# Memory loaded already transposed, its normalisation moved behind the key and value projections, in a one-layer hybrid decoder kernel

## The chip, the core and the metric

The kernel runs on one core of a Trainium2 chip. The metric is the device time of one execution in microseconds (us). The core has five engines with instruction queues of their own: TensorE (PE, the matrix products; its weight loads are shown as PEld), VectorE (DVE), ScalarE (ACT), GpSimd (POOL) and SyncE (SP, which here only issues DMA transfers). Each works through its queue strictly in order and waits on semaphores for the others. Matrix products accumulate in PSUM banks; everything else lives in the on-chip SBUF.

## The reference

One decoder layer over 1024 tokens of width 1024: a mixer (pooling and gated linear attention), a cross-attention over 256 memory tokens, a convolutional feed-forward part, each on an RMS-normalised input. The part that the change touches is the memory side of the cross-attention:

```python
def rms_norm(x, w):
    y = x32 * lax.rsqrt(jnp.mean(x32 * x32, axis=-1, keepdims=True) + EPS)
    return (y * w.astype(jnp.float32)).astype(x.dtype)

def memory_cross_attention(h, mem_n, wq, wkv, wo):      # mem_n = rms_norm(mem, norm_mem_w)
    q = (h @ wq).reshape(b, s, XATTN_HEADS, XATTN_HEAD_DIM)
    kv = mem_n @ wkv
    k = kv[..., :D_MODEL]; v = kv[..., D_MODEL:]
    ...
```

The inverse root mean square of a memory token is one factor for a whole row of `mem_n`. It can therefore be applied before the product with `wkv` or after it.

## The kernel before

Float32 products are made of three passes: every operand is split into a high part (a copy in the type fp32r) and a low part (the rest), and `mm3` (L89 to L92) issues high x high, high x low and low x high. `split` (L94) makes the two parts: ACT writes the high one (L96, or L99 where a row factor is given as scale), DVE the low one (L97, or L100). `wunit` (L114) does the same for half a weight chunk: ACT at L122, DVE at L123. So every K chunk needs two ACT and two DVE instructions of 128x512 before TensorE can use it.

**The head of the program.** The keys K and values V of the memory come first, because their input is small: `mem` is 256 x 1024. The two row tiles of `mem` are loaded; ACT squares and sums each row (L297, `inv_rms`), POOL adds EPS and takes the power -0.5 (L298, L299), DVE multiplies by the row factor and the gain `norm_mem_w` (L514; the gain was spread over the partitions by two products with a row of ones, L507); TensorE turns the result round in 128x128 blocks against an identity (`put_T`, L307, transposes at L312), and `split` writes it into `att["m"]`, the operand that all key and value products share.

Then `J["km"]` makes K feature block by feature block: eight blocks f0 to f7, each of 24 matmuls of 128x256 into one PSUM bank of the pool `psA` (5 banks), each with a 512 KB chunk of `wkv`. `kmem_evac` (L446) splits the bank into `att["K"]`. `J["vm"]` makes V: two halves of 48 matmuls of 128x512, from eight more chunks of 512 KB. K is not read before the cross-attention, far later.

Between these products stands other work for which the mixer waits: four token tiles of `x` (x0 to x3) are normalised by `normed` (ACT L297, POOL L298 and L299, DVE L304), transposed on TensorE (two groups of four transposes for a tile, L312, into the 3 banks of the pool `psB`) and split into `hmix[0]` (L96, L97). The order on each engine is fixed when the program is built: a scheduler places the instructions, and `pin` holds some of them in the order in which they are written. All loads of the head go through the DMA queue of SP in the order written. After V comes `J["vg", 0]`, the first product of the mixer, and from there on the program is a long stream of products.

Names in the rows: `pa` a bank of psA, `pb` of psB, `w` a split weight half, `r` a split operand, `f` a large SBUF tile, `t` a small one, `s` a column of row factors.

Of the kernel before, what the change touches and what calls it, by code (L numbers as in the profile page):

```python
# [8 lines left out]
F32 = mybir.dt.float32  # L9
F32R = mybir.dt.float32r  # L10
AF = mybir.ActivationFunctionType
ALU = mybir.AluOpType
# [3 lines left out]
P = 128  # L16
T = 1024
D = 1024
KT = D // P
TB = 512  # L20
NB = T // TB
M = 256
DFF = 2816
NF = DFF // P
EPS = 1e-6
WINDOWS = (2, 4, 8, 16)
HALO = 16
HK = KT // 2
# [13 lines left out]
@with_exitstack  # L42
def hybrid_layer(ctx: ExitStack, tc: tile.TileContext, x, mem, norm_mix_w, w_in, pool_w, pool_scale,
                 gk_w2, gk_b, gla_norm_w, w_out, norm_xattn_w, norm_mem_w, wq, wkv, wo,
                 norm_ffn_w, w_up, conv_w, conv_b, w_down, norm_final_w, out):
    nc = tc.nc

    const = ctx.enter_context(tc.tile_pool(name="const", bufs=1))
# [9 lines left out]
    pin = tc.keep_in_program_order  # L58
# [3 lines left out]
    def nm(s):  # L62
        uid[0] += 1
        return f"{s}{uid[0]}"

    def f4(*shape):
        return big.tile([P, *shape], F32, tag="big", name=nm("f"))

    def r4(*shape):
        return big.tile([P, *shape], F32R, tag="big", name=nm("r"))  # L70
# [4 lines left out]
    def sc(n):  # L75
        return small.tile([P, n], F32, tag="small", name=nm("s"))

    def bankA():
        return psA.tile([P, 512], F32, tag="psA", name=nm("pa"))

    def bankB():
        return psB.tile([P, 512], F32, tag="psB", name=nm("pb"))
# [11 lines left out]
    def split(dst, src, scale=None):  # L94
        if scale is None:
            nc.scalar.activation(dst.hi, src, AF.Copy)  # L96
            nc.vector.tensor_tensor(dst.lo, src, dst.hi.bitcast(F32), ALU.subtract)  # L97
        else:
            nc.scalar.activation(dst.hi, src, AF.Copy, scale=scale)  # L99
            nc.vector.scalar_tensor_tensor(dst.lo, src, scale, dst.hi.bitcast(F32), ALU.mult, ALU.subtract)  # L100
# [46 lines left out]
    early, issues = [False], []  # L147
# [19 lines left out]
    ws = Stream()  # L167
# [57 lines left out]
    def proj_tok(banks, feat, nk, step_k, n):  # L225
        for kc in range(0, nk, step_k // 2):
            w = ws.take()
            for i, ps in enumerate(banks):
                for kk in range(step_k // 2):
                    a = feat.k(kc + kk)  # L230
                    mm3(ps, a[:, i * P:(i + 1) * P], w[:, kk, :], kc + kk == 0, kc + kk == nk - 1)
                    yield n * 3 / 2400
# [42 lines left out]
    halfneg = const.tile([P, 4], F32, name="halfneg")  # L275
    nc.gpsimd.memset(halfneg, -0.5)

    def dma(dst, src):
        ins = nc.sync.dma_start(out=dst, in_=src)
        if starting or pinned:  # L280
            pin(ins)

    def bcast_row(src, q=nc.gpsimd):
        w = f4(D)
        ins = q.dma_start(out=w, in_=src.partition_broadcast(P))
        if starting:
            pin(ins)
        return w

    def load_x(t):  # L290
        xt = f4(D)
        dma(xt, x[t * P:(t + 1) * P, :])
        return xt

    def inv_rms(xt, junk):
        ss, rs = sc(1), sc(1)
        nc.scalar.activation(junk, xt, AF.Square, scale=1.0 / 32, accum_out=ss)  # L297
        nc.gpsimd.tensor_scalar(ss, ss, EPS, None, ALU.add)  # L298
        nc.gpsimd.tensor_tensor(rs, ss, halfneg[:, 0:1], ALU.pow)  # L299
        return rs  # L300

    def normed(xt, wb, pool=None):
        y = pool.tile([P, D], F32, tag="y", name=nm("y")) if pool else f4(D)
        nc.vector.scalar_tensor_tensor(y, xt, inv_rms(xt, y), wb, ALU.mult, ALU.mult)  # L304
        return y

    def put_T(xn, feat, c0):  # L307
        pss = []
        for q in range(2):
            ps = bankB()  # L310
            for j in range(4):
                nc.tensor.transpose(ps[:, j * P:(j + 1) * P], xn[:, (4 * q + j) * P:(4 * q + j + 1) * P], ident)  # L312
            pss.append(ps.rearrange("p (k c) -> p k c", k=4))
            feat.put(4 * q, 4, c0, P, pss[q])
        return pss
# [128 lines left out]
    att = {}  # L444

    def kmem_evac(f, ps):  # L446
        if f == 0:
            att["K"] = Feat(M)
        att["K"].put(f, 1, 0, M, ps.unsqueeze(1))

    def vmem_gen():
        V = att["V"] = [Pair(r4(D), r4(D)) for _ in range(2)]
        for half in range(2):
            banks = [bankA() for _ in range(2)]
            yield from proj_tok(banks, att["m"], KT, 2, 512)
            for i in range(2):
                split(V[i][:, half * 512:(half + 1) * 512], banks[i])

    hx, oo = [None, None], [None, None]

# [8 lines left out]
    J = {}  # L469
    early[0] = True  # L470
    J["km"] = feat_job(wkv, 0, 8, lambda: att["m"], kmem_evac, M)
    J["vm"] = job([rows(wkv, kc, 2, D + half * 512, 512) for half in range(2) for kc in range(0, KT, 2)], vmem_gen)
    early[0] = False
    for b in range(NB):
# [20 lines left out]
    def load_m(i):  # L495
        mt = f4(D)
        dma(mt, mem[i * P:(i + 1) * P, :])
        return mt

    ones, row = f4(P), f4(D)  # L500
    nc.vector.memset(ones[0:1, :], 1.0)
    mts = [load_m(0)]
    dma(row[0:1, :], norm_mem_w.rearrange("(o c) -> o c", o=1))
    mts.append(load_m(1))
    wb_mem = [bankA(), bankA()]
    for half in range(2):
        nc.tensor.matmul(wb_mem[half], ones[0:1, :], row[0:1, half * 512:(half + 1) * 512], start=True, stop=True)  # L507
    att["m"] = Feat(M)
    xn = [f4(D), f4(D)]
    for xt, y in zip(mts, xn):  # L510
        rs = inv_rms(xt, y)
        for half in range(2):
            hs = slice(half * 512, (half + 1) * 512)
            pin(nc.vector.scalar_tensor_tensor(y[:, hs], xt[:, hs], rs, wb_mem[half], ALU.mult, ALU.mult))  # L514
    for k in range(2):
        issues[k]()
    ws.load(1)
    xts = [load_x(0)]
    wb_mix = bcast_row(norm_mix_w, nc.sync)
    for i in range(1, 4):  # L520
        issues[i + 1]()
        xts.append(load_x(i))
    put_T(xn[0], att["m"], 0)
    ws.load(2)
    put_T(xn[1], att["m"], P)
    ws.load(2)
    hmix[0] = Feat(TB)


# [355 lines left out]
    for i in range(4):  # L885
# [4 lines left out]
        xn = normed(xres[4 + i], wb_f, ybuf)  # L890
# [301 lines left out]
    for j in list(plan):  # L1192
# [7 lines left out]
_INS = ["x", "mem", "norm_mix_w", "w_in", "pool_w", "pool_scale", "gk_w2", "gk_b", "gla_norm_w", "w_out",  # L1200
        "norm_xattn_w", "norm_mem_w", "xattn_wq", "xattn_wkv", "xattn_wo", "norm_ffn_w", "ffn_w_up",
        "ffn_conv_w", "ffn_conv_b", "ffn_w_down", "norm_final_w"]


# [18 lines left out]
```

## Time and profile before

| what | value |
|---|---|
| median of 3 runs | 1296.89 us (1296.56 to 1297.16) |
| the profiled execution | 1294.73 us |
| its span on the core | 1292.8 us |
| TensorE busy in the span | 1260.8 us (98%) |
| VectorE / ScalarE / GpSimd busy | 885.0 / 645.9 / 222.2 us |
| first K matmul / first V matmul | at 11.88 us / at 41.66 us of the span |

The span runs from the first to the last instruction on the core; the execution's own time has 1.9 us more around it. The profile is of one execution, the median of others. A share of busy time is a mean over stages with different limits: what a change in the head of the program is worth is read from the first 42 us, not from the 98%.

### The profile page before, as it was taken

The numbers are of one execution on the slowest core, as the hardware profiler recorded it, in microseconds if no ns is written. First come the engines' busy times: TensorE is split into PE (matmuls) and PEld (weight loads), VectorE is DVE, ScalarE is ACT, GpSimd is POOL, SyncE is SP. The second block draws the span as 40 slices with busy tenths as digits, with TensorE's granted clock in tenths as the row PEclk, the third lists the DMA queues.
The fourth block names the chain that finished last, engine by engine and source line by source line (L and its number), as shares of the span: only waits on it lengthen the run. The fifth ranks groups of instructions, "written<-read, shape, count | busy, mean of one in ns | idle before, by whom it ended". The sixth has DMA issues, their size and how long they took to land.

```text
span 1292.8 us, 16765 instructions
## 1 busy us (share of the span) xinstructions
PE 1260.8 (98%) x6326; PEld 1063.2 (82%) x6326; DVE 885.0 (68%) x1331; ACT 645.9 (50%) x1169; POOL 222.2 (17%) x238
## 2 busy tenths in 40 slices
PE   8999999999999999999889999999999999999997
PEld 7898878988788899998777888888888887888885
DVE  6723686236757554446887787778778778999865
ACT  6636544364446443345555555555545544474453
POOL 2000110001200000010113443443443420000002
PEclk9999999999999999999999999999999999999998
DMA  9333225332142212233322322232232246876202
GB/s 288 137 100 83 75 98 197 88 80 79 61 151 66 66 50 82 66 112 134 119 76 82 98 86 66 94 98 65 82 98 82 65 150 241 286 251 188 82 22 108
DMA packets 140271, 143.93 MB, mean 111 GB/s; under 512 B 4696, under 2 KB 112926, under 8 KB 140191
## 3 DMA queue, kind: packets, MB, share of 16 engines
q1 hardware_dynamic: 138031, 136.05, 32.9%
q0 software_dynamic: 1584, 5.77, 1.3%
q8 instruction: 49, 0.80, 0.3%
q10 hardware_dynamic: 576, 1.05, 0.2%
q14 instruction: 31, 0.25, 0.1%
HBM read 122.93 MB, written 19.92 MB: 111 GB/s over the span
## 4 chain that ended last, share of the span: by engine, by line
PE 69%; issue 16%; DVE 6%; DMA 4%; ACT 3%; POOL 1%; SPq 0%; POOLq 0%; ACTq 0%; DVEq 0%
PE pa L918 9%; PE pa L920 8%; PE pa L919 8%; PE pa L92 8%; PE pa L90 8%; PE pa L91 8%; PE pb L918 5%; PE pb L920 5%; PE pb L919 5%; DMA f<-gd 2%; DVE r L97 2%; DVE w L123 1%; PE pb L312 1%; DVE w L97 1%; DMA wr<-in_ffn_w_up_dram 1%
## 5 line engine op out<-in xcount | busy, mean ns | idle before, releaser
L123 DVE TENSOR_TENSOR w<-wr,w 128x512 fp32r<-128x512 f32 (+1 forms) x222 | 179.5, 811 | 179.2 <-ACT w L122 178.6
L122 ACT ACTIVATE w<-wr 128x512 fp32r<-128x512 f32 (+1 forms) x222 | 139.0, 628 | 134.0 <-PE pa L92 112.1
L918 PE MATMUL pa<-r,w 128*128 128x512 f32 x400 | 158.2, 396 | 9.6 <-ACT f L811 5.0
L90 PE MATMUL pa<-w,r 128*128 128x512 f32 (+2 forms) x480 | 159.3, 332 | 0.1
L91 PE MATMUL pa<-w,r 128*128 128x512 f32 (+2 forms) x480 | 157.4, 328 | 0.3 <-DVE w L123 0.3
L919 PE MATMUL pa<-r,w 128*128 128x512 f32 x400 | 157.4, 393 | 0.0
L920 PE MATMUL pa<-r,w 128*128 128x512 f32 x400 | 157.3, 393 | 0.0
L92 PE MATMUL pa<-w,r 128*128 128x512 f32 (+2 forms) x480 | 156.8, 327 | 0.2 <-DVE r L97 0.2
L90 PE MATMUL pa<-r,w 128*128 128x512 f32 (+1 forms) x384 | 149.3, 389 | 0.7 <-ACT r L96 0.7
L92 PE MATMUL pa<-r,w 128*128 128x512 f32 (+1 forms) x384 | 143.9, 375 | 0.2 <-DVE w L123 0.2
L91 PE MATMUL pa<-r,w 128*128 128x512 f32 (+1 forms) x384 | 143.9, 375 | 0.0
L918 PEld LDWEIGHTS pa<-r,w 128*128 128x128 f32 x400 | 76.3, 191 | 27.1 <-ACT f L811 6.6
L92 PEld LDWEIGHTS pa<-w,r 128*128 128x128 f32 x480 | 90.7, 189 | 8.9 <-DVE r L97 1.1
L90 PEld LDWEIGHTS pa<-w,r 128*128 128x128 f32 x480 | 90.9, 189 | 7.7 <-ACT w L122 0.4
L91 PEld LDWEIGHTS pa<-w,r 128*128 128x128 f32 x480 | 90.8, 189 | 7.6 <-DVE w L123 0.5
L920 PEld LDWEIGHTS pa<-r,w 128*128 128x128 f32 x400 | 76.1, 190 | 16.2 <-DVE w L123 0.2
L919 PEld LDWEIGHTS pa<-r,w 128*128 128x128 f32 x400 | 76.3, 191 | 15.8
L122 ACT ACTIVATE w<-ws 128x512 fp32r<-128x512 f32 x88 | 53.4, 626 | 71.7 <-POOL ws L959 29.4
L90 PEld LDWEIGHTS pa<-r,w 128*128 128x128 f32 x384 | 73.2, 191 | 14.0 <-issue 1.6
L918 PE MATMUL pb<-r,w 128*128 128x512 f32 x216 | 84.0, 389 | 0.0
L919 PE MATMUL pb<-r,w 128*128 128x512 f32 x216 | 84.0, 389 | 0.0
L920 PE MATMUL pb<-r,w 128*128 128x512 f32 x216 | 84.0, 389 | 0.0
(225 smaller groups left out, 2665.6 us busy)
## 6 DMA issues: line engine op xcount, KB each, us to landing
wr<-in_ffn_w_up_dram SPq DMA_DIRECT2D x47, 512.0 KB, 3.8
wr<-in_ffn_w_down_dram SPq DMA_DIRECT2D x33, 512.0 KB, 3.7
wr<-in_w_in_dram SPq DMA_DIRECT2D x24, 512.0 KB, 4.0
gd<-f SPq DMA_DIRECT2D x22, 512.0 KB, 3.0
f<-gd SPq DMA_DIRECT2D x22, 512.0 KB, 5.8
f<-in_xattn_wkv_dram SPq DMA_DIRECT2D x16, 512.0 KB, 8.2
f<-in_x_dram SPq DMA_DIRECT2D x16, 512.0 KB, 7.4
wr<-in_w_out_dram SPq DMA_DIRECT2D x16, 512.0 KB, 3.6
```

Of the source, the lines that this page charges most:

```text
L90: nc.tensor.matmul(ps, l.hi, r.hi, start=start, stop=False)
L91: nc.tensor.matmul(ps, l.hi, r.lo, start=False, stop=False)
L92: nc.tensor.matmul(ps, l.lo, r.hi, start=False, stop=stop)
L97: nc.vector.tensor_tensor(dst.lo, src, dst.hi.bitcast(F32), ALU.subtract)
L122: ia = nc.scalar.activation(w.hi, src, AF.Copy)
L123: ib = nc.vector.tensor_tensor(w.lo, src, w.hi.bitcast(F32), ALU.subtract)
L312: nc.tensor.transpose(ps[:, j * P:(j + 1) * P], xn[:, (4 * q + j) * P:(4 * q + j + 1) * P], ident)
L918: nc.tensor.matmul(ps, l.hi, r.hi, start=start, stop=False, **kw)
L919: nc.tensor.matmul(ps, l.hi, r.lo, start=False, stop=False, **kw)
L920: nc.tensor.matmul(ps, l.lo, r.hi, start=False, stop=stop, **kw)
```

## The change

The host hands over two more arrays: `memT`, the memory transposed, and `wmemT`, the gain laid out as 128 x 8. The kernel loads `memT` straight into the layout of `att["m"]`; ACT and DVE split it with the gain as scale (L99, L100), without the row factor. So the transposes of the memory, the products with ones and the multiplications at L514 go. The row factors are still worked out from the two row tiles of `mem` (ACT L524, POOL L525 and L526) and are applied to the results: to V as a scale in `split`, since there a token is a partition; to K, where a token is a column, by a DVE product of each bank with a 128x256 tile `att["rs"]` that holds the 256 factors in every partition (L450). That tile is made by way of DRAM: POOL issues a transfer that writes the 128x2 factors to a DRAM tile `rsd`, waits for it, and issues a second one that reads them back into all 128 partitions. The loads are written in another order: the first chunk of `wkv` leads, then `memT`, the second chunk, `mem`, and so on.

```diff
@@ kmem_evac, vmem_gen
-        att["K"].put(f, 1, 0, M, ps.unsqueeze(1))
+        k = t2(M)
+        nc.vector.tensor_tensor(k, ps, att["rs"], ALU.mult)
+        att["K"].put(f, 1, 0, M, k.unsqueeze(1))
...
-                split(V[i][:, half * 512:(half + 1) * 512], banks[i])
+                split(V[i][:, half * 512:(half + 1) * 512], banks[i], att["rsm"][:, i:i + 1])
...
-    ones, row = f4(P), f4(D)
-    nc.vector.memset(ones[0:1, :], 1.0)
-    mts = [load_m(0)]
-    dma(row[0:1, :], norm_mem_w.rearrange("(o c) -> o c", o=1))
-    mts.append(load_m(1))
-    wb_mem = [bankA(), bankA()]
-    for half in range(2):
-        nc.tensor.matmul(wb_mem[half], ones[0:1, :], row[0:1, half * 512:(half + 1) * 512], start=True, stop=True)
-    att["m"] = Feat(M)
-    xn = [f4(D), f4(D)]
-    for xt, y in zip(mts, xn):
-        rs = inv_rms(xt, y)
-        for half in range(2):
-            hs = slice(half * 512, (half + 1) * 512)
-            pin(nc.vector.scalar_tensor_tensor(y[:, hs], xt[:, hs], rs, wb_mem[half], ALU.mult, ALU.mult))
-    for k in range(2):
-        issues[k]()
-    ws.load(1)
+    wm = sc(KT)
+    pin(nc.scalar.dma_start(out=wm, in_=wmemT))
+    mT = [f4(HK, M) for _ in range(2)]
+    issues[0]()
+    for j in range(2):
+        dma(mT[j], memT[j * 512:(j + 1) * 512, :].rearrange("(k p) m -> p k m", p=P))
+    issues[1]()
+    mts = [load_m(0), load_m(1)]
+    issues[2]()
+    issues[3]()
     xts = [load_x(0)]
     wb_mix = bcast_row(norm_mix_w, nc.sync)
+    att["m"] = Feat(M)
+    rsm = att["rsm"] = sc(2)
+    for j in range(2):
+        ws.load(j + 1)
+        for k in range(HK):
+            att["m"].put(HK * j + k, 1, 0, M, mT[j][:, k:k + 1, :], wm[:, HK * j + k:HK * j + k + 1])
+    for i, mt in enumerate(mts):
+        ss = sc(1)
+        pin(nc.scalar.activation(mt, mt, AF.Square, accum_out=ss))
+        pin(nc.gpsimd.tensor_scalar(ss, ss, 1.0 / D, EPS, ALU.mult, ALU.add))
+        pin(nc.gpsimd.tensor_tensor(rsm[:, i:i + 1], ss, halfneg[:, 0:1], ALU.pow))
+    dram0 = ctx.enter_context(tc.tile_pool(name="dram0", bufs=1, space=bass.MemoryType.DRAM))
+    rsd = dram0.tile([2, P], F32, name="rsd", tag="rsd")
+    att["rs"] = f4(M)
+    pin(nc.gpsimd.dma_start(out=rsd.rearrange("i p -> p i"), in_=rsm))
+    pin(nc.gpsimd.dma_start(out=att["rs"], in_=rsd.rearrange("i p -> (i p)").partition_broadcast(P)))
+    ws.load(4)
     for i in range(1, 4):
-        issues[i + 1]()
+        issues[i + 3]()
         xts.append(load_x(i))
-    put_T(xn[0], att["m"], 0)
-    ws.load(2)
-    put_T(xn[1], att["m"], P)
-    ws.load(2)
```

With the sources, the order on the engines changes, in their first hundred or so rows; behind these every engine has the same order as before. Three places follow.

ACT, the head of its queue, before: the squares of `mem` (f_89, f_92) lead, then the first weight halves.

```order
L297 ACTIVATE f_102,s_104<-f_89 128x1024
L297 ACTIVATE f_103,s_111<-f_92 128x1024
L122 ACTIVATE w_122<-f_118 128x512
L96 ACTIVATE r_98<-pb_141 128x4x128
```

The same place now (f_90 and f_94 are the first two chunks of `wkv`, f_88 and f_89 the halves of `memT`, f_96 and f_98 the rows of `mem`):

```order
L505 DMA s_86<-in_wmemT_dram 128x8
L122 ACT_TABLE_LOAD
L122 ACTIVATE w_113<-f_90 128x512
L99 ACTIVATE r_108<-f_88,s_86 128x256 x4
L122 ACTIVATE w_124<-f_90 128x512
L99 ACTIVATE r_109<-f_89,s_86 128x256 x4
L524 ACTIVATE f_96,s_135<-f_96 128x1024
L524 ACTIVATE f_98,s_139<-f_98 128x1024
L122 ACTIVATE w_149<-f_94 128x512
```

The squares now stand between the weight halves of the first and of the second chunk.

DVE, the normalisation of x0 to x3 (L304 writes f_225, f_300, f_391 and f_486), before: the tiles are spread among the weight halves and the splits of the K banks pa_232 (f0), pa_269 (f1), and so on.

```order
L123 TENSOR_TENSOR w_248<-f_120,w_248 128x512
L304 SCALAR_TENSOR_TENSOR f_225<-f_125,s_227,f_127 128x1024
L97 TENSOR_TENSOR r_265<-pa_232,r_263 128x256
...
L304 SCALAR_TENSOR_TENSOR f_300<-f_131,s_302,f_127 128x1024
L97 TENSOR_TENSOR r_265<-pa_269,r_263 128x256
...
L304 SCALAR_TENSOR_TENSOR f_391<-f_135,s_393,f_127 128x1024
L97 TENSOR_TENSOR r_265<-pa_327,r_263 128x256
```

Now (L304 writes f_220, f_291, f_386 and f_481; pa_450 is the bank of f5, pa_510 of f6; t_256 to t_411 are f0 to f3 after the product with the row factors):

```order
L450 TENSOR_TENSOR t_506<-pa_450,f_146 128x256
L304 SCALAR_TENSOR_TENSOR f_220<-f_104,s_222,f_106 128x1024
L97 TENSOR_TENSOR r_254<-t_256,r_252 128x256
...
L304 SCALAR_TENSOR_TENSOR f_291<-f_157,s_293,f_106 128x1024
L97 TENSOR_TENSOR r_171<-pb_298,r_167 128x2x128
L450 TENSOR_TENSOR t_543<-pa_510,f_146 128x256
...
L304 SCALAR_TENSOR_TENSOR f_386<-f_161,s_388,f_106 128x1024
L97 TENSOR_TENSOR r_174<-pb_402,r_170 128x2x128
...
L304 SCALAR_TENSOR_TENSOR f_481<-f_165,s_483,f_106 128x1024
```

All four normalisations stand behind the evacuation of f5. Between the first two are four splits of K, between the second and the third seven splits and the evacuation of f6, between the last two four splits.

PE, the transposes of x0 to x3, before: a tile's eight stand behind every second K block; f6 is pa_513 and f7 pa_548.

```order
L92 MATMUL pa_269<-r_99,w_248 128x256
L312 MATMUL pb_307<-ident,f_225 128x128 x4
L312 MATMUL pb_316<-ident,f_225 128x128 x4
L90 MATMUL pa_327<-r_98,w_270 128x256
...
L312 MATMUL pb_493<-ident,f_391 128x128 x4
L312 MATMUL pb_502<-ident,f_391 128x128 x4
L312 MATMUL pb_581<-ident,f_486 128x128 x4
L90 MATMUL pa_513<-r_98,w_456 128x256
```

Now (f6 is pa_510, f7 pa_547, V begins with pa_606):

```order
L312 MATMUL pb_298<-ident,f_220 128x128 x4
L312 MATMUL pb_307<-ident,f_220 128x128 x4
L92 MATMUL pa_510<-r_109,w_466 128x256
...
L312 MATMUL pb_393<-ident,f_291 128x128 x4
L312 MATMUL pb_402<-ident,f_291 128x128 x4
L312 MATMUL pb_488<-ident,f_386 128x128 x4
L312 MATMUL pb_497<-ident,f_386 128x128 x4
L312 MATMUL pb_580<-ident,f_481 128x128 x4
L312 MATMUL pb_589<-ident,f_481 128x128
L90 MATMUL pa_547<-r_108,w_513 128x256
```

The transposes of x0 stand within f6, and those of x1, x2 and x3 in one run between f6 and f7, so the 24 matmuls of f7 and all of V are queued behind them. The matmuls of f0 to f5 follow each other with nothing between.

## Rows read from the trace of the kernel before

**Rows 1.** The page, busy time of an engine in the span.

```profile
PE 1260.8 (98%) x6326; PEld 1063.2 (82%) x6326; DVE 885.0 (68%) x1331; ACT 645.9 (50%) x1169; POOL 222.2 (17%) x238
```

**Rows 2.** Busy time of each engine in two stretches, TensorE's clock, DMA share, GB/s.

```profile
0.00:41.66 41.66, 35.97 (x244) 32.41 (x245) 29.35 (x53) 27.33 (x58) 8.30 (x45) 1.00 0.97 309
41.66:1292.80 1251.14, 1224.80 (x6085) 1030.82 (x6083) 855.68 (x1279) 618.53 (x1112) 213.91 (x193) 0.99 0.33 105
```

**Rows 3.** TensorE's waits from 60 us on: total us, times, longest.

```profile
PE pa L918 <- ACT f L811: 5.0, 2, 3.8
```

**Rows 4.** Timeline of TensorE in the head: start us, us, what, [idle before].

```profile
8.31 2.88 PE L312 MATMUL pb<-ident,f 128*128 128x128 f32 x12
11.88 0.58 PE L90 MATMUL pa<-r,w 128*128 128x256 f32 x1 [0.69 <-ACT r L96]
...
14.39 0.41 PE L91 MATMUL pa<-r,w 128*128 128x256 f32 x1
14.60 0.41 PE L92 MATMUL pa<-r,w 128*128 128x256 f32 x1
...
26.61 0.28 PE L92 MATMUL pa<-r,w 128*128 128x256 f32 x1
26.73 1.03 PE L312 MATMUL pb<-ident,f 128*128 128x128 f32 x8
27.52 0.36 PE L90 MATMUL pa<-r,w 128*128 128x256 f32 x1
...
41.66 0.48 PE L90 MATMUL pa<-w,r 128*128 128x512 f32 x1
```

**Rows 5.** Timeline of ACT, its first waits for loads of 512 KB.

```profile
4.53 1.06 ACT L297 ACTIVATE f<-f 128x1024 f32<-128x1024 f32 x1 [2.46 <-DMA f<-in_mem_dram]
...
5.88 1.06 ACT L297 ACTIVATE f<-f 128x1024 f32<-128x1024 f32 x1 [0.20 <-DMA f<-in_mem_dram]
...
7.69 0.63 ACT L122 ACTIVATE w<-f 128x512 fp32r<-128x512 f32 x1 [0.66 <-DMA f<-in_xattn_wkv_dram]
```

**Rows 6.** Groups from 12.9 to 41.7 us: count, busy us, mean ns, idle before.

```profile
L123 DVE TENSOR_TENSOR w<-f,w 128x512 fp32r<-128x512 f32 x18 | 12.0, 684 | 0.2
L122 ACT ACTIVATE w<-f 128x512 fp32r<-128x512 f32 x17 | 10.5, 632 | 0.7 <-PE pa L92 0.7
L97 DVE TENSOR_TENSOR r<-pb,r 128x256 fp32r<-128x256 f32 x14 | 5.5, 417 | 0.0
L304 DVE SCALAR_TENSOR_TENSOR f<-f,s,f 128x1024 f32<-128x1024 f32 x4 | 5.1, 1285 | 4.2 <-POOL s L299 4.2
...
L96 ACT ACTIVATE r<-pb 128x256 fp32r<-128x256 f32 x14 | 4.9, 385 | 1.6 <-DVE r L97 1.5
L297 ACT ACTIVATE f<-f 128x1024 f32<-128x1024 f32 x4 | 4.2, 1050 | 0.0
```

**Rows 7.** Timeline, normalisation of the last tile of x.

```profile
30.95 1.05 ACT L297 ACTIVATE f<-f 128x1024 f32<-128x1024 f32 x1
...
32.48 0.57 POOL L299 TENSOR_TENSOR s<-s,halfneg 128x1 f32<-128x1 f32 x1
33.08 1.28 DVE L304 SCALAR_TENSOR_TENSOR f<-f,s,f 128x1024 f32<-128x1024 f32 x1 [1.57 <-POOL s L299]
```

**Rows 8.** Transfers issued from POOL: count, KB each, median us to landing.

```profile
xd<-f POOLq DMA_DIRECT2D x8, 512.0 KB, 4.4
f<-in_norm_ffn_w_dram POOLq DMA_DIRECT2D x1, 512.0 KB, 7.7
```

**Rows 9.** Stretches around a gap on TensorE, columns as in the second group.

```profile
638.50:640.80 2.30, 0.07 (x1) 0.00 (x0) 2.30 (x6) 0.97 (x3) 0.00 (x0) 1.00 0.31 90
640.80:643.10 2.30, 0.00 (x0) 0.00 (x0) 2.21 (x6) 1.78 (x6) 0.00 (x0) 0.51 0.46 138
643.10:647.60 4.50, 4.45 (x11) 3.44 (x12) 4.47 (x11) 4.50 (x13) 0.00 (x0) 0.50 0.43 126
647.60:652.00 4.40, 4.40 (x21) 3.64 (x20) 3.87 (x10) 1.99 (x6) 0.00 (x0) 0.99 0.37 109
```

More of the change, by code (lines that the diff above doesn't have):

```diff
@@ L44, in hybrid_layer @@
                  gk_w2, gk_b, gla_norm_w, w_out, norm_xattn_w, norm_mem_w, wq, wkv, wo,
-                 norm_ffn_w, w_up, conv_w, conv_b, w_down, norm_final_w, out):
+                 norm_ffn_w, w_up, conv_w, conv_b, w_down, norm_final_w, memT, wmemT, out):
     nc = tc.nc
@@ L1202 @@
         "ffn_conv_w", "ffn_conv_b", "ffn_w_down", "norm_final_w"]
+_MORE = {"memT": lambda g: g["mem"][0].T, "wmemT": lambda g: g["norm_mem_w"][0].reshape(KT, P).T}
 def kernel(**inputs):
@@ L1217 @@
         args.append(nc.dram_tensor(f"in_{name}_dram", a.shape, mybir.dt.from_np(a.dtype), kind="ExternalInput").ap())
+    for name, lay in _MORE.items():
+        a = arrays[f"in_{name}_dram"] = _np.ascontiguousarray(lay({k: _np.asarray(v) for k, v in inputs.items()}))
+        args.append(nc.dram_tensor(f"in_{name}_dram", a.shape, mybir.dt.from_np(a.dtype), kind="ExternalInput").ap())
     args.append(nc.dram_tensor("out_0_dram", (T, D), F32, kind="ExternalOutput").ap())
```

## The prediction

> **What bounds the kernel now.** I read the page first: TensorE is busy for 98% of the span [rows 1], so time is won or lost where it waits or works slowly. The table of two stretches then divides the span at the first matmul of V, at 41.66 us. Ahead of it TensorE is busy for 35.97 us of 41.66 and the transfers are busy for 0.97 of the time; behind it TensorE is busy for 1224.80 of 1251.14 us and the transfers for 0.33 [rows 2]. From 60 us on the longest group of its waits is 5.0 us in two pieces, for ACT [rows 3]; no group there names a transfer. Hence a shift of V's start goes through to the end unchanged: the rest has the same order, waits for nothing that comes at a fixed time, and has no slack to take up a delay. The question is where V starts.
>
> The timeline of TensorE shows how 41.66 us come about. The first K matmul starts at 11.88 us, behind twelve transposes from 8.31 on. There the clock is at its lower level of 1.2 GHz: matmuls of 256 columns start 0.21 us apart (14.39, 14.60), later 0.12 us apart (26.61, 26.73) at 2.4 GHz, and eight transposes take 0.79 us (26.73 to 27.52) [rows 4]. A K block of 24 matmuls is thus 5.1 us at the lower level and 2.9 at the upper one. Eight blocks (23.0) and 32 transposes of x (3.2) are 26.2 us; from 11.88 to 41.66 are 29.8. So before, K runs with almost nothing lost, because the normalised tiles of x arrive between the blocks as they are needed.
>
> **The change, part by part: the start.** A load of 512 KB in whole rows lands 1.35 us behind the one ahead of it, a wkv chunk 1.81 us behind; the first lands at 4.53 [rows 5]. In the new order of loads I get: chunk 0 at 5.0, the halves of memT at 6.6 and 8.1 (their pieces lie between the two kinds: 1.58 each), chunk 1 at 9.9, the rows of mem at 11.3 and 12.6. The L99 copy and L100, of 128x256, are like the splits of that size, 0.39 and 0.42 us [rows 6]. So f0 starts at 7.0 instead of 11.88: a gain of 4.9 us, with the memory's transposes, L507 and L514 off the path. At the lower clock f0 ends at 12.1.
>
> Then the first new wait. On ACT the weight halves of f1 (L122) stand behind both squares of mem. The second square can start at 12.6, takes 1.05 us [rows 6], and the half-chunk another 0.63 [rows 6]: f1 starts at 14.3, 2.2 us after f0, though its chunk landed at 9.9. With five blocks of 2.9 us, f5 ends at 28.8; if the clock stays low through f1 it ends 2.2 us later, if it does not, nothing is lost. I take the middle, as no row tells which level a block behind such a gap gets: f5 ends at 29.9. The chunks do not hold it: chunk 4 comes by the same sums at 20.7, chunk 5 at 23.9.
>
> **The normalisation of x, now on the path.** f7 and V are queued behind the transposes of x1, x2 and x3, and DVE normalises x0 only behind the evacuation of f5. From there, with the durations of [rows 6]:
> - evacuation 0.42, L304 of x0 1.29, four splits of K at 0.42, L304 of x1 1.29: 4.7 us.
> - ACT squares x2 only behind the copies of x1's second group of transposes. With three psB banks that group needs the bank of x0's first group back: transposes 0.4, a copy 0.39, two DVE splits 0.84, transposes 0.4, a copy 0.39: 2.4 us.
> - from the start of a square to the start of its L304 are 2.13 us (30.95 to 33.08) [rows 7], and 1.29 for x2's: 3.4 us.
> - four splits, L304 of x3: 3.0 us. Its first transposes, a bank released by copy and split, the second group: 1.3 us.
>
> That is 14.8 us; successive instructions overlap a little, so I take 14.4, and f7 starts at 44.3. TensorE finishes f6 at about 33.7 (29.9, a block and the first eight transposes); from there to 44.3 it has 24 transposes, 2.4 us of work, and waits for some 8 us.
>
> At the upper clock f7 ends and V starts at 47.2, 5.5 us later than 41.66. But in a gap like this the granted clock falls: near 638.5 TensorE went idle and the clock was at 0.5 from 640.8 to 647.6, although matmuls ran again from 643.1 on [rows 9]; f7 would lie in such a stretch. It then takes 5.1 instead of 2.9 us, and the last transposes, 0.24 us each there (2.88 for twelve) [rows 4], cost 0.6 more: V starts at 50.0, 8.3 us later. I take this end, since the gap on TensorE in [rows 9] is shorter than the one here.
>
> **The way through DRAM.** The factors are ready 2.1 us after the second square can start (30.95 to 33.05, the end of L299) [rows 7]: at 14.7. Two transfers issued by POOL follow, the second waiting for the first. No row shows one of this size; the nearest are loads and stores of 512 KB, 4.4 us as a rule and 7.7 among others [rows 8]. I take 4.4 twice, because smaller ones have less to move, yet the queues are full here: the tile is there at 23.5. What hides it: DVE's first product with it stands ahead of the low weight half of f4. f4 starts at 24.1 and needs that half with its third matmul; two products (0.42) and a split (0.68) [rows 6] go ahead, so the tile may come at 22.8. 0.7 us late, which pass to the end, as all later work on DVE waits behind. At 7.7 each it is there at 30.1, 7.3 late; if they took less than 4.0 each nothing would be late, and nothing gained either, since f4 waits for f3 in any case.
>
> By the Trainium skill, "DMA: Bandwidth & Descriptors", section "Anatomy of one DMA", a transfer from GpSimd costs about 2.0 us and its bytes, here an estimated 4.3 us for both; the tile would then come at 19.0 and the sum be 8.3 instead of 9.0. The rows are above that figure, for larger transfers.
>
> The other edits are off the path: the product L450 adds eight DVE instructions of 0.42, of which those of f0 to f4 lie under matmuls and f5's and f6's are in the sum; L99 and L100 for V take the place of L96 and L97 of the same shape; the gain column (4 KB, from ACT) has until 6.6 to arrive, and if it were late f0 would be, by as much. The extra 1 MB of loads is some 3 us of transfers, but V uses a chunk only every 2.6 us and [rows 2] shows 0.33 of transfer time behind 41.66.
>
> **Sum.** 8.3 + 0.7 = 9.0 us. The profiled execution would take 1294.73 + 9.0 = 1303.7; the median shown lies 2.16 above that execution, so 1296.89 + 9.0 = 1305.9.
>
> **Rivals.**
> - The way through DRAM decides. For it: the factors are written as single elements, and the transfers of the head are at 0.97. Against: little is moved. At 7.7 each, 8.3 + 7.3 gives 1312.5; it tells from a tile that comes after about 26. A rule of the Trainium skill stands behind it (same page, "Rules for kernel authors"): a last dimension that is not contiguous costs a descriptor for each element. No row here shows such a write.
> - The clock does not fall, because the transposes in the run keep it up, or it rises before f7: 5.5 + 0.7, 1303.1. Against: behind the twelve transposes from 8.31 on the matmuls still ran at 0.21 [rows 4].
> - Faster: the normalisations keep ahead of TensorE after all. Then only the early start counts: 4.9 us, 1292.0. It decides whether x3 is normalised before f6 ends, near 34; by the sum above it is near 43, so ACT and DVE would have to do 13 us of queued work in 4.
> - No change: the stages behind V take up the delay. That needs a wait there for something that does not move with V; [rows 3] has none of a size above 5.0, and that one is for ACT.
>
> **How the numbers follow.** The chain of x with the low clock: 0.62. The DRAM way deciding: 0.20. Clock kept: 0.08. Faster 0.05, no change 0.05. A difference of 0.2% (2.6 us) is about what a measurement of this kernel can tell from no change; the first three are all slower by more: 0.90. The range goes from the case with the clock kept, less 1.6 us for the first landings and the overlaps, which I chose (1301.5), to the late tile (1312).
>
> **What would show it.** Right: the first K matmul near 7; a gap of about 2 us ahead of f1 released by ACT; f0 to f6 without gaps; then some 10 us in which TensorE does only transposes, waiting for DVE at L304 and L97; f7 with matmuls 0.21 apart; the first 512-column matmul near 51. If TensorE waits ahead of f4 and the wait of DVE's first L450 ends on the POOL transfer after 23, the DRAM way has a share. Wrong: V's first matmul below 41.7, or a later stage that ends at its old time.

## The result and the profile after

The changed kernel takes 1316.05 us (median of four runs, 1314.26 to 1319.49), the kernel before 1297.03 beside it: a ratio of 1.0158, 95% interval 1.0138 to 1.0177. It is slower, as forecast, but by 19.0 us and not by 9.0. The profiled execution took 1314.26 us with a span of 1312.4, against 1294.73 and 1292.8 before.

The page's line of busy times answers to [rows 1]: TensorE does the same work in a span that is 19.6 us longer.

```profile
PE 1261.2 (96%) x6306; PEld 1065.4 (81%) x6306; DVE 884.1 (67%) x1338; ACT 647.9 (49%) x1173; POOL 224.3 (17%) x240
```

The two stretches of [rows 2], divided at the first matmul of V, which now comes at 61.53 us (start, length, TensorE's busy time; the last three columns are the clock, the DMA share and GB/s):

```profile
0.00:61.53 61.53, 36.42 (x224) 34.21 (x225) 29.91 (x59) 29.03 (x62) 10.25 (x47) 0.83 0.82 240
61.53:1312.40 1250.87, 1224.79 (x6084) 1031.14 (x6082) 854.21 (x1279) 618.91 (x1111) 214.03 (x193) 0.99 0.32 104
```

The second stretch is as long as before (1250.87 against 1251.14), with the same busy time. So everything was lost ahead of V, 19.9 us, and nothing came back behind it. The timeline of TensorE up to there, its waits (in brackets: idle before, and what ended it) and V's first matmul:

```profile
6.87 0.58 PE L90 MATMUL pa<-r,w 128*128 128x256 f32 x1 [6.87 <-ACT r L99]
14.34 0.38 PE L90 MATMUL pa<-r,w 128*128 128x256 f32 x1 [1.97 <-ACT w L122]
35.48 0.58 PE L92 MATMUL pa<-r,w 128*128 128x256 f32 x1 [10.04 <-DVE w L123]
53.23 1.94 PE L312 MATMUL pb<-ident,f 128*128 128x128 f32 x8 [4.16 <-DVE f L304]
61.53 0.40 PE L90 MATMUL pa<-w,r 128*128 128x512 f32 x1
```

The first two rows stand where the prediction put them, and the fourth is the wait for the normalisation of x that it described. The third is new in its size: the third matmul of f4 waits 10.04 us for the low weight half. On DVE that half stands behind the first two products with the spread factors, and these wait for the tile that comes by way of DRAM. The timelines of DVE and POOL, and the groups of DMA issues from 15 to 34 us (KB, us to landing):

```profile
34.08 0.76 DVE L450 TENSOR_TENSOR t<-pa,f 128x256 f32<-128x256 f32 x2 [13.22 <-DMA f<-rsd]
34.75 0.68 DVE L123 TENSOR_TENSOR w<-f,w 128x512 fp32r<-128x512 f32 x1
```

```profile
15.00 0.96 POOL L530 DMA_DIRECT2D rsd<-s  x1 [0.31 <-POOL s L526]
26.91 0.59 POOL L531 DMA_DIRECT2D f<-rsd  x1 [10.96 <-DMA rsd<-s]
```

```profile
f<-rsd POOLq DMA_DIRECT2D x1, 128.0 KB, 7.1
rsd<-s POOLq DMA_DIRECT2D x1, 1.0 KB, 11.6
```

The write of 1 KB takes 11.6 us and the read-back 7.1, where [rows 8] had led me to 4.4 each: the tile is there at 34.05, not at 23.5. From 21 us on, while the write is still in progress, the other loads almost stop. The stretches of 2 us (columns as above), answering to a rate of 309 GB/s in [rows 2]:

```profile
19.00:21.00 2.00, 2.00 (x19) 2.00 (x19) 0.69 (x1) 0.63 (x1) 0.00 (x0) 1.00 1.22 352
21.00:23.00 2.00, 2.00 (x19) 2.00 (x18) 0.00 (x0) 0.00 (x0) 0.00 (x0) 1.00 1.32 34
23.00:25.00 2.00, 2.00 (x19) 2.00 (x18) 0.00 (x0) 1.10 (x2) 0.00 (x0) 1.00 1.07 145
25.00:27.00 2.00, 0.45 (x4) 0.24 (x3) 0.00 (x0) 0.05 (x1) 0.09 (x1) 1.00 1.07 212
```

Packets are under way throughout (shares of 1.07 to 1.32; the share adds up the time that packets take, and so can lie above 1), yet only 34 GB/s move from 21 to 23 us. The kernel before also has 39 GB/s in that stretch, but at a share of 0.17, with few packets under way; the fair comparison is e1, with the loads in the order of the changed kernel.

### The profile page after: what moved, and what is told of

The parts are those of the page before. It is cut to its first block, busy times and chain, and to the rows that moved or that the text cites. A ratio compares the mean times of both kernels' runs of the same rounds, so it can differ in the third digit from the quotient of the medians.

```text
span 1312.4 us, 16741 instructions
## 1 busy us (share of the span) xinstructions
PE 1261.2 (96%) x6306; PEld 1065.4 (81%) x6306; DVE 884.1 (67%) x1338; ACT 647.9 (49%) x1173; POOL 224.3 (17%) x240
## 4 chain that ended last, share of the span: by engine, by line
PE 67%; issue 16%; DVE 6%; DMA 5%; ACT 3%; SPq 2%; POOL 1%; POOLq 0%; ACTq 0%; DVEq 0%
PE pa L927 8%; PE pa L929 8%; PE pa L928 8%; PE pa L90 7%; PE pa L92 7%; PE pa L91 7%; PE pb L927 5%; PE pb L929 5%; PE pb L928 5%; SPq L279 2%; DMA f<-gd 2%; DVE r L97 2%; DVE w L123 1%; PE pb L312 1%; DVE w L97 1%
## 5 line engine op out<-in xcount | busy, mean ns | idle before, releaser
L90 PE MATMUL pa<-r,w 128*128 128x512 f32 (+1 forms) x384 | 151.4, 394 | 8.8 <-ACT r L99 6.9
L92 PE MATMUL pa<-r,w 128*128 128x512 f32 (+1 forms) x384 | 146.3, 381 | 10.3 <-DVE w L123 10.3
L91 PE MATMUL pa<-r,w 128*128 128x512 f32 (+1 forms) x384 | 146.0, 380 | 0.0
L927 PEld LDWEIGHTS pa<-r,w 128*128 128x128 f32 x400 | 76.3, 191 | 26.4 <-ACT f L820 5.9
L92 PEld LDWEIGHTS pa<-r,w 128*128 128x128 f32 x384 | 75.2, 196 | 23.6 <-DVE w L123 10.7
L90 PEld LDWEIGHTS pa<-r,w 128*128 128x128 f32 x384 | 75.5, 197 | 21.9 <-ACT r L99 6.9
L929 PEld LDWEIGHTS pa<-r,w 128*128 128x128 f32 x400 | 76.1, 190 | 16.2 <-DVE w L123 0.2
L928 PEld LDWEIGHTS pa<-r,w 128*128 128x128 f32 x400 | 76.4, 191 | 15.8
L91 PEld LDWEIGHTS pa<-r,w 128*128 128x128 f32 x384 | 75.4, 196 | 12.4 <-issue 1.0
L927 PE MATMUL pb<-r,w 128*128 128x512 f32 x216 | 84.0, 389 | 0.0
```

The source lines that it names most:

```text
L90: nc.tensor.matmul(ps, l.hi, r.hi, start=start, stop=False)
L91: nc.tensor.matmul(ps, l.hi, r.lo, start=False, stop=False)
L92: nc.tensor.matmul(ps, l.lo, r.hi, start=False, stop=stop)
L927: nc.tensor.matmul(ps, l.hi, r.hi, start=start, stop=False, **kw)
L928: nc.tensor.matmul(ps, l.hi, r.lo, start=False, stop=False, **kw)
L929: nc.tensor.matmul(ps, l.lo, r.hi, start=False, stop=stop, **kw)
```

## The experiments

Three causes were possible for the ten missing microseconds and for the nine that had been forecast: the wait for the tile (theory T), the order of the x normalisation (O), and the slowing of the other loads (J). The runs in one table; "above" is the median less that of the kernel before in the same comparison, and V's first matmul is at 41.66 before and at 61.53 in the changed kernel. Single executions of the kernel before lie between 1292.29 and 1298.57 us in these comparisons, so "above" is good to 1 or 2 us. "V starts" is from the one profiled execution of each run.

| run | median us | above | ratio, 95% interval | V starts |
|---|---|---|---|---|
| e1, no transfers | 1304.64 | 10.0 | 1.0076, 1.0058 to 1.0094 | 51.2 |
| e2, transfers unused | 1307.84 | 13.2 | 1.0101, 1.0080 to 1.0121 | 54.1 |
| e3, x in program order | 1311.73 | 17.1 | 1.0132, 1.0108 to 1.0156 | 60.2 |
| e4, spread by TensorE, x in order | 1298.66 | 4.0 | 1.0031, 1.0019 to 1.0043 | 47.7 |
| e5, two pieces of 512 B | 1309.12 | 12.9 | 1.0097, 1.0081 to 1.0113 | 55.6 |
| e6, 128 pieces of 8 B | 1311.79 | 15.6 | 1.0116, 1.0100 to 1.0132 | 58.5 |
| e7, before with both transfers | 1307.48 | 11.3 | 1.0080, 1.0063 to 1.0096 | 52.4 |
| e8, a version of my own | 1296.86 | 0.6 | 1.0002, 0.9994 to 1.0011 | 38.4 |
| e9, no transfers, x in order | 1298.45 | 2.5 | 1.0019, 1.0008 to 1.0029 | 46.6 |
| e10, before with the write | 1300.74 | 4.8 | 1.0043, 1.0027 to 1.0059 | 46.1 |
| e11, write issued by ACT | 1318.52 | 22.6 | 1.0172, 1.0154 to 1.0191 | 62.9 |

**e1: without the transfers.**

```diff
-    pin(nc.gpsimd.dma_start(out=rsd.rearrange("i p -> p i"), in_=rsm))
-    pin(nc.gpsimd.dma_start(out=att["rs"], in_=rsd.rearrange("i p -> (i p)").partition_broadcast(P)))
+    pin(nc.gpsimd.memset(att["rs"], 1.0))
```

> This kernel leaves out K's row factors: the tile that multiplies K's blocks is set to one, the two transfers by way of DRAM are gone, and all else stays in the order of the changed kernel. Theory T (the way through DRAM holds the first eviction and through it the fourth block of K for about 10.5 of the 19.6 us): the wait of 10.04 us of the fourth block is gone, what stays is the late normalisation of x, V starts near 51 and the kernel takes 1304.5 to 1307. Rival O (the order of the x normalisation costs it all, the late tile is only covered by it): 1313 to 1316, V starts near 60. Rival J (the element-wise write slows the other loads and that is the larger part of the loss): as T or lower, and the stretch from 21 to 23 us moves about 300 GB/s where it moved 34.

It took 10.0 us more than before, V started at 51.16. In the same stretch of 21 to 23 us the loads ran at full rate, and behind f6 TensorE waited for the x normalisation and then worked at the lower level of its clock, 1.2 GHz: f7's matmuls take 0.41 us, as those at the lower level in [rows 4], and the stretch from 45 to 50 us has 0.50.

```profile
21.00:23.00 2.00, 2.00 (x19) 2.00 (x18) 1.08 (x2) 0.78 (x2) 0.00 (x0) 1.00 1.17 326
45.00:50.00 5.00, 4.94 (x24) 4.54 (x22) 4.17 (x9) 3.73 (x10) 0.00 (x0) 0.50 0.77 261
```

```profile
40.96 1.94 PE L312 MATMUL pb<-ident,f 128*128 128x128 f32 x8 [3.45 <-DVE f L304]
46.23 0.41 PE L91 MATMUL pa<-r,w 128*128 128x256 f32 x1
```

So without the way through DRAM 9.0 of the 19.0 us go, and O as the only cause falls. One thing did not stay as expected: x is not held in program order here, and without the transfers the scheduler normalises x0 ahead of the evacuation of f5 and no longer behind it, and puts its transposes behind 137 matmuls of K, where the changed kernel has 161. The 9.0 us may hold a share of that; e5 below bounds it.

**e2: the transfers without the wait for them.**

```diff
+    idle = f4(M)
+    pin(nc.gpsimd.memset(att["rs"], 1.0))
-    pin(nc.gpsimd.dma_start(out=att["rs"], in_=rsd.rearrange("i p -> (i p)").partition_broadcast(P)))
+    pin(nc.gpsimd.dma_start(out=idle, in_=rsd.rearrange("i p -> (i p)").partition_broadcast(P)))
```

> The two transfers are issued as in the changed kernel but land in a tile that nothing reads; K's blocks are multiplied by a tile set to one (K's row factors are left out). T with the wait alone as the cost: as the kernel without the transfers, 1304.5 to 1307. J (the transfers slow the loads of weights and x beside them): 2 to 5 us above the kernel without the transfers, 1307 to 1311, with the fall of the rate to some 34 GB/s still there. O: 1313 to 1316.

3.2 us above e1: the four runs of each do not overlap (1303.09 to 1306.74 and 1306.89 to 1309.88), the intervals of the ratios do. The write took 12.2 us, the rate fell again, and ACT had to wait for weight chunks that had been on time:

```profile
21.00:23.00 2.00, 2.00 (x16) 2.00 (x16) 1.12 (x2) 0.74 (x2) 0.00 (x0) 0.83 1.48 61
23.00:25.00 2.00, 2.00 (x19) 2.00 (x18) 1.13 (x3) 1.15 (x2) 0.00 (x0) 1.00 1.12 73
```

```profile
28.90 1.15 ACT L122 ACTIVATE w<-f 128x512 fp32r<-128x512 f32 x2 [3.94 <-DMA f<-in_xattn_wkv_dram]
33.55 1.05 ACT L297 ACTIVATE f<-f 128x1024 f32<-128x1024 f32 x1
```

The second row is the square of x0, which stands behind the halves of f6 on ACT. In e1, where only one of these two is ahead of it, it came 5.3 us earlier:

```profile
28.25 1.04 ACT L297 ACTIVATE f<-f 128x1024 f32<-128x1024 f32 x1
```

TensorE starts f6 no later than in e1 (33.18 us, 33.49 there), but f7 at 49.51 instead of 45.85: the time is lost in the normalisation of x, not in the blocks of K.

The order of x here is that of the changed kernel (x0 behind the evacuation of f5, its transposes behind 159 matmuls of K), so the wait for the tile is shown: 5.8 us, 19.0 less 13.2. The other 3.2 are J together with the order by which e1 differs. e10 shows J by itself in the kernel before.

**e3 and e9: the order of the x normalisation, with and without the transfers.** Both hold ACT's square and DVE's scaling of x where the program has them, in the same order in both; e9 also lacks the transfers.

```diff
-        nc.scalar.activation(junk, xt, AF.Square, scale=1.0 / 32, accum_out=ss)
+        ia = nc.scalar.activation(junk, xt, AF.Square, scale=1.0 / 32, accum_out=ss)
+        if starting:
+            pin(ia)
...
-        nc.vector.scalar_tensor_tensor(y, xt, inv_rms(xt, y), wb, ALU.mult, ALU.mult)
+        ib = nc.vector.scalar_tensor_tensor(y, xt, inv_rms(xt, y), wb, ALU.mult, ALU.mult)
+        if starting:
+            pin(ib)
```

> The way through DRAM stays, but the squares and scalings of x are held in program order, so that the transposes of x stand between K's blocks as in the kernel before and not between its seventh and eighth. T: the late tile still holds the first eviction to 34, so that little is won, 1311 to 1315. O: the loss is mostly gone, 1305 or less.

> No transfers (K's row factors are left out, the tile is set to one) and the x normalisation held in program order. If the 10.0 us that stayed without the transfers are the order of the x normalisation: as the version with the factors spread by TensorE in this order or up to 2 us better, since TensorE's four spreading matmuls and their waits are gone too: 0 to 4 us above the kernel before. If they are something else (the weights of the second block behind the squares, the loads): 8 us or more above.

Without the transfers the order is worth 7.5 us (10.0 in e1, 2.5 in e9). What stays in e9 are mainly these waits of TensorE, and a clock at 0.50 from 15 to 21 us:

```profile
14.11 0.46 PE L90 MATMUL pa<-r,w 128*128 128x256 f32 x1 [2.07 <-ACT w L122]
22.60 1.09 PE L316 MATMUL pb<-ident,f 128*128 128x128 f32 x8 [1.33 <-DVE f L306]
```

With the transfers the order gains only 1.9 (19.0 and 17.1), which is not clear of the noise, for the wait then strikes earlier: DVE stands still from 15.5 us on at its first product, ACT behind it at the first split of K, and so already f2, and not only f4, is without weights. DVE, ACT and TensorE of e3:

```profile
33.94 0.76 DVE L454 TENSOR_TENSOR t<-pa,f 128x256 f32<-128x256 f32 x2 [18.48 <-DMA f<-rsd]
```

```profile
34.40 0.42 ACT L96 ACTIVATE r<-t 128x256 fp32r<-128x256 f32 x1 [15.96 <-DVE t L454]
```

```profile
35.39 0.58 PE L90 MATMUL pa<-r,w 128*128 128x256 f32 x1 [16.21 <-ACT w L122]
```

So the two costs cover each other in part: repairing the order alone shows little, although it is worth 7.5 us once the tile is on time.

**e4: both undone.** The order as in e3, and the factors spread by TensorE.

```diff
+    ps = bankB()
+    for i in range(2):
+        pin(nc.vector.tensor_scalar(dg[:, i * P:(i + 1) * P], ident, rsm[:, i:i + 1], None, ALU.mult))
+        nc.tensor.matmul(ps[:, i * P:(i + 1) * P], ones, dg[:, i * P:(i + 1) * P], start=True, stop=True)
+    pin(nc.vector.tensor_copy(att["rs"], ps[:, 0:M]))
```

> Both are undone: the row factors are spread by two matmuls of TensorE (ones times a diagonal of the factors) and an eviction instead of DRAM, and the x normalisation is held in program order. T and O together as two terms (10.5 and some 8.5 us of 19.6): V starts near 47, the kernel takes 1299 to 1303, that is 2 to 6 us above the kernel before. If the early start of the first block of K is kept to the end: 1292 to 1296. If the transposes of x between K's blocks bring waits of their own: 1304 or more.

1298.66, 4.0 above before: of the 19.0 us 15.0 are gone. It is still not faster, though its first K matmul comes at 7.36 instead of 11.88: TensorE waits for the factors and for x0, and from 15 to 20 us it runs at 1.2 GHz, where the kernel before had 2.4.

```profile
13.76 0.49 PE L538 MATMUL pb<-f,f 128*128 128x128 f32 x2 [1.24 <-DVE f L537]
15.10 0.80 PE L538 MATMUL pb<-f,f 128*128 128x128 f32 x2 [0.85 <-DVE f L537]
23.73 1.09 PE L316 MATMUL pb<-ident,f 128*128 128x128 f32 x8 [1.47 <-DVE f L306]
```

```profile
15.00:20.00 5.00, 4.22 (x18) 3.92 (x19) 2.00 (x5) 2.50 (x5) 0.80 (x2) 0.50 1.09 360
```

**e5, e6 and e11: why the write takes 11.6 us.** e5 turns the factors on TensorE and writes two pieces of 512 bytes; e6 writes them as they lie, 128 pieces of 8 bytes; e11 keeps the 256 elements of 4 bytes, but issues the write from ACT.

Of e5, e6 and e11 in turn:

```diff
+    nc.tensor.transpose(ps[0:2, 0:P], rsm, ident)
+    pin(nc.vector.tensor_copy(rsr[0:2, :], ps[0:2, 0:P]))
+    pin(nc.gpsimd.dma_start(out=rsd, in_=rsr[0:2, :]))
```

```diff
+    rsd = dram0.tile([P, 2], F32, name="rsd", tag="rsd")
+    pin(nc.gpsimd.dma_start(out=rsd, in_=rsm))
```

```diff
+    pin(nc.scalar.dma_start(out=rsd.rearrange("i p -> p i"), in_=rsm))
```

> The row factors are first turned on TensorE into two rows of 128 and written to DRAM as two pieces of 512 bytes from GpSimd's queue, and read back as in the changed kernel; everything else is as there. Theory S (the write of 256 single elements of 4 bytes is what takes 11.6 us and what slows the other loads): the first transfer takes 4.4 us or less, no stretch falls to 34 GB/s, the tile is there at 22 to 26, the kernel takes 1303 to 1308, as without the transfers (10 us above before). Rival Q (any transfer of this queue waits that long, since the loads fill the DMA engines): the first transfer takes 10 us or more, the tile comes at 34 or later, 1312 to 1317.

> The row factors are written to DRAM as they lie on the partitions, 128 pieces of 8 bytes where there were 256 of 4 bytes, and VectorE reads the spread tile with a stride. If the price goes by the number of pieces: the first transfer takes 6 to 8 us where it took 11.6, the slow stretch is half as long, the tile comes at 29 to 31, the kernel takes 1308 to 1313. If it goes by the queue (Q): as changed, 1313 to 1317. If only elements of 4 bytes are slow: 1303 to 1308.

> As changed, but the write of the 256 elements is issued from ScalarE's queue, about 1 us later; the read-back stays on GpSimd's. If GpSimd's queue is what makes the write slow: it lands in 6 us or less, the tile is there by 29, and the kernel takes 7 to 13 us more than the kernel before. If it is the elements and the full DMA engines, whatever the queue: 10 to 13 us to land, the fall to 34 GB/s is there again, and the kernel takes 15 to 22 us more than before.

The groups of DMA issues of e5, then of e6:

```profile
f<-rsd POOLq DMA_DIRECT2D x1, 128.0 KB, 6.1
rsd<-f POOLq DMA_DIRECT2D x1, 1.0 KB, 5.5
```

```profile
f<-rsd POOLq DMA_DIRECT2D x1, 128.0 KB, 6.8
rsd<-s POOLq DMA_DIRECT2D x1, 1.0 KB, 7.8
```

The same 1 KB takes 5.5 us in 2 pieces, 7.8 in 128, 11.6 in 256. With two pieces the loads go on at 324 GB/s from 21 to 23 us; with 128 they move 307 in that stretch, and dip to 228 only from 23 to 25 us, when the write has landed (at 22.57). e6 kept within its ranges for the pieces (the tile lands at 29.7), and its products with strided reads take no longer (419 ns, 420 in the changed kernel). From ACT it is no faster: POOL, which waits for the write, issues the read-back at 27.93, 12.9 us behind ACT's issue, and the loads fall to 27 GB/s. Its 22.6 us above lie a little over the 15 to 22 expected, as the tile landed at 35.7.

```profile
15.00 0.43 ACTq L531 DMA_DIRECT2D rsd<-s  x1
```

```profile
27.93 0.77 POOL L532 DMA_DIRECT2D f<-rsd  x1 [12.96 <-DMA rsd<-s]
```

So the write pays for being cut up, from either queue, and even in two pieces it takes 5.5 us here, not the 4.4 or less that I expected. e5 missed its 1303 to 1308 by 1.1 us: 5.5 + 6.1 still bring the tile only at 27.6, and f4 waits:

```profile
29.32 0.39 PE L92 MATMUL pa<-r,w 128*128 128x256 f32 x1 [2.92 <-DVE w L123]
```

e5 also tells what e1's other order is worth, for it has the order of x of the changed kernel and loads at full rate. Its V starts at 55.6; less this wait, and less 1.4 us that the rest of f4 took longer behind it (22 matmuls in 4.1 us, 2.6 at 0.12 apart), that is an estimated 51.2, as in e1. So the other order of e1 is worth little by this estimate, and J is about 3 us in the changed kernel; no run separates the two.

That the number of pieces decides, rather than their size in bytes, is not separated: both change together from e5 to the changed kernel, and in e5 the write also comes from 2 partitions instead of 128.

**e7 and e10: the transfers in the kernel before.** e7 adds both, into a tile that nothing reads; e10 adds the write alone.

```diff
+        rsl.append(rs)
...
+    for i in range(2):
+        pin(nc.gpsimd.tensor_scalar(rsm[:, i:i + 1], rsl[i], 1.0, None, ALU.mult))
+    pin(nc.gpsimd.dma_start(out=rsd.rearrange("i p -> p i"), in_=rsm))
```

and in e7 also

```diff
+    pin(nc.gpsimd.dma_start(out=idle, in_=rsd.rearrange("i p -> (i p)").partition_broadcast(P)))
```

> The kernel before with both transfers added (256 elements of 4 bytes out, 128 rows back, into a tile that nothing reads) and nothing else changed. What the transfers cost the other loads alone: the unused transfers cost 3.2 us in the order of the changed kernel, so 1295 to 1299 here, with a stretch of some 6 us behind the write at a third of the rate of the loads or less. If the loads have that much slack in this order: within 0.2% of the kernel before. If the loss of the changed kernel is mainly this: 1303 or more.

> The kernel before with the write of 256 elements of 4 bytes alone added, without the read-back, so that nothing waits on GpSimd's queue. If the 11.3 us of the kernel before with both transfers came from the read-back's issue, which held GpSimd's queue till 22.4 us and the factors of x0 behind it: 0 to 3 us above the kernel before, although the loads still fall to about 100 GB/s for some 6 us. If they came from the slow loads: 7 us or more above.

Both cost more than I expected. e7's 11.3 us have a second cause that I had overlooked: the read-back's issue waits on POOL until 22.40 for the write, and the factors of x0 (L298, L299), which were made at 15.6 before, stand behind it, with 3.2 us of POOL's small set-up instructions between; TensorE then waits 8.13 us for x0.

```profile
8.71 0.96 POOL L531 DMA_DIRECT2D rsd<-s  x1 [0.31 <-POOL s L527]
22.40 0.59 POOL L532 DMA_DIRECT2D f<-rsd  x1 [12.73 <-DMA rsd<-s]
26.23 0.22 POOL L298 TENSOR_SCALAR s<-s 128x1 f32<-128x1 f32 x1
```

```profile
28.57 1.94 PE L312 MATMUL pb<-ident,f 128*128 128x128 f32 x8 [8.13 <-DVE f L304]
```

e10, without that queue, gives the price of the slowed loads in this order: 4.8 us, above my 0 to 3. The write took 12.4 us and the rate fell as in the changed kernel, so the loads of x1 and of the weights came late. The stretches, and ACT's wait for x1:

```profile
15.00:17.00 2.00, 2.00 (x13) 2.00 (x13) 1.23 (x3) 1.11 (x3) 0.92 (x2) 1.00 2.14 107
17.00:19.00 2.00, 2.00 (x19) 2.00 (x18) 2.00 (x4) 0.90 (x2) 0.00 (x0) 1.00 0.84 70
```

```profile
21.45 1.06 ACT L297 ACTIVATE f<-f 128x1024 f32<-128x1024 f32 x1 [3.08 <-DMA f<-in_x_dram]
```

**e8: a version meant to be faster than both.** As e4, but the rows of mem come after the third weight chunk, their squares and the spreading behind f1, the first three K banks wait in PSUM, and the transposes of x start with f4 and reach into V.

```diff
+        held.append((f, ps))
+        if f == 1:
+            spread_rows[0]()
+        if f > 1:
+            for g, pg in held:
...
+    weave(norm_feat([lambda i=i: xts[i] for i in range(4)], wb_mix, hmix[0], 5.0, 7.0, 6.0))
```

> A version meant to keep the early start: the row factors are spread by TensorE, the rows of the memory are loaded, squared and summed after the third weight chunk and behind the second block of K, the first three blocks of K wait in PSUM for the factors, x is normalised in program order and its transposes stand from the fourth block of K on into V. If the theory of two terms is whole: no wait of TensorE over 2 us behind the first block of K, V starts between 38 and 41 (41.7 before), and the kernel takes 1290 to 1294, faster than before by 1 to 5 us. If new waits for weights or a low granted clock take the gain: 1295 to 1300.

V starts at 38.44, 3.2 us earlier than before, with no wait above 1.2 us, and yet the time is that of the kernel before (1.0002, 0.9994 to 1.0011). The expected 1290 to 1294 were missed. A part of the work had only changed places: two tiles of x are transposed inside V now, and TensorE's waits are many small ones. From 40 to 60 us it was busy for 20.00 us before, for 18.67 now (first row before, second e8):

```profile
40.00:60.00 20.00, 20.00 (x99) 16.82 (x98) 13.16 (x23) 10.97 (x21) 0.00 (x0) 1.00 0.19 66
40.00:60.00 20.00, 18.67 (x87) 14.36 (x87) 15.71 (x29) 12.70 (x27) 0.78 (x2) 1.00 0.39 139
```

Of the 3.8 us between the earlier start (3.2) and the result (0.6 above), these 1.33 us and the 16 transposes, some 1.6 us by [rows 4], make up 2.9; the rest stays open. I found no version that beats the kernel before.

## Why the prediction was wrong by ten microseconds

**The step that failed is the size of the way through DRAM**: "I take 4.4 twice, because smaller ones have less to move". The two took 11.6 and 7.1 us. The tile came at 34.05 instead of 23.5, 10.5 us later, and the time missed the forecast by 10.0. The mechanism was there, with its place (DVE's first product ahead of f4's low half, f4's third matmul), but as a rival with a chance of 0.20, and the upper price that I gave it, 7.7 each, was still below what the write took. The range ended at 1312, below the 1312.5 that I had worked out for that rival myself. In the sum the way through DRAM had 0.7 us; by e1 it costs 9.0. That is 8.3 of the 10.0 missed; the other 1.7 are e1's 10.0 against the 8.3 of the sum without the tile. The rows that the 4.4 was taken from, [rows 8], are of 512 KB in large pieces, issued far behind the head. I went by bytes, and so took the smaller transfer for no dearer than the larger; e5 and e6 show that the cutting into pieces counts. The rule of the Trainium skill that stood behind that rival ("DMA: Bandwidth & Descriptors", section "Rules for kernel authors": a last dimension that is not contiguous becomes one descriptor for each element) agrees with e11, where the write of 256 elements shows as 272 packets on ACT's queue (number, MB, share):

```profile
q10 hardware_dynamic: 272, 0.00, 1.2%
```

On POOL's queue the packets do not tell: both transfers together are 80 there, with 2, 128 or 256 pieces. The estimate from the Trainium skill's section "Anatomy of one DMA" of the same page, 4.3 us for both transfers, does not agree: they took 18.7, and even with two pieces 5.5 + 6.1; the measurement decides.

**A second effect was not in the sum at all:** the write slows the loads beside it. It is worth about 3 us here (e2 against e1, with the estimate from e5) and 4.8 in the order of the kernel before (e10). I had priced the loads' lateness only by the bytes added, and put the chunks of f4 and f5 at 20.7 and 23.9; in the changed kernel ACT waits for them until 23.90 and 28.17.

**The other steps held to within 2 us.** In the order of the prediction:
- f0 at 6.87 (forecast 7.0); f1 at 14.34 behind a wait of 1.97 for ACT (14.3 and 2.2), as the squares of mem stand ahead of its halves. f1 itself took 5.0 us, 14.34 to 19.30, where I had taken 4.0 as the middle of the two levels, so f4 began at 25.05 instead of 24.1. Which level a block behind this gap gets still cannot be told: f1 took from 3.5 us (e6) to 6.6 (e2) in the profiled executions.
- Behind the wait of 10.04 us the clock was low again, which no term had: f4's matmuls start 0.21 us apart until 39.07, some 1.4 us more than at 0.12.

```profile
35.00:37.00 2.00, 1.51 (x7) 1.52 (x8) 2.00 (x5) 0.00 (x0) 0.00 (x0) 0.50 0.65 183
```

- The chain of x: from the evacuation of f5 at 42.93 to f7's first matmul at 57.06 are 14.1 us; I had 14.4.
- The clock fell in the run of waits, to 0.50 from 52.86 to 59.68, and f7 took 4.5 us (5.1; 2.9 at 2.4 GHz): it rose within f7, so this term was 0.6 too large. The waits between f6 and f7 are 5.9 us in all (0.49, 0.65, 4.16, 0.59), where I had some 8.
- The order by itself: e1, with the transfers gone, starts V at 51.2, against 50.0 by the sum without the tile, and takes 10.0 us more than before, against 8.3. e9 shows that 7.5 of these are the order; the other 2.5 are the waits in front of f1 and of the transposes of x and the low clock behind them, less the early start.
- Nothing behind V gives anything back: its second stretch differs by 0.3 us.

One way to divide the 19.0 us, in the order in which the runs take the parts away: 5.8 the wait for the tile, 3.2 the slowed loads, 7.5 the order of x, 2.5 the rest. The 3.2 and the 7.5 rest on e1, whose order of x lies between that of the changed kernel and that of e9. The division holds for this sequence only, as e3 shows: with the transfers in place the order is worth 1.9.

## What to carry to other kernels

Price a transfer by how it is cut up, not by its bytes alone, and by a row of a like kind beside like loads: the read-back of 128 KB took 5.7 to 7.8 us in the head, the 512 KB of [rows 8] 4.4 as a rule far behind it (no run here issues the same transfer in both places); where no such row exists, let the range reach well above the dearest row at hand. A spread over partitions by way of DRAM is two transfers one behind the other: name what stands behind the first reader on its engine, and behind the issue of the second on its queue, before moving it into the head of a program whose loads are at full rate. When two delays lie on one path, undo both before judging either; e3 alone would have cleared the order of a cost of 7.5 us.

## What the runs showed of the hardware

- A write of 1 KB to DRAM in 256 elements of 4 bytes took 11.6 to 13.4 us here (e2, e3, e7, e10 and the changed kernel), and cut the loads beside it from some 330 GB/s to less than 160 for 4 to 8 us; the lowest stretch of 2 us had 12 (e3), 27 (e11), 34 (the changed kernel), 61 (e2) and 70 to 73 (e10, e7). Packets stayed under way meanwhile (shares of 0.8 to 2.1 in e10; 0.43 and 0.54 in the lowest stretches of e3 and e11). As 128 pieces of 8 bytes it took 7.8, as two of 512 bytes 5.5, and from 15 us to their landing no stretch of 2 us lay below 307. Issued from ACT instead of POOL it was as slow (12.9).
- The loads are cut late: in e10 the write is issued at 9.25 us, and the rate falls only from 15 us on; in the changed kernel the two are at 15.00 and about 21. That would fit a write that first waits about as long as the 5.5 us of e5's, and then hinders the rest; it is not shown, for no view here tells what happens within the DMA engines in that time.
